# Low parts of split weights: an accumulating DMA in place of VectorE's subtraction, in a two-layer hybrid encoder

## The chip, the cores and the metric

The kernel runs on one core of one Trainium2 chip. The metric is the time of one execution on the device, in microseconds (us). Engines: TensorE (PE; its weight loads are PEld), VectorE (DVE), ScalarE (ACT), GpSimd (POOL) and SyncE (SP), which here only issues DMAs.

## The reference, cut to what matters

Two layers over 512 tokens of width 1024. Each layer is a half-step SwiGLU, a mixer of three parallel head groups, and a second half-step SwiGLU with a gated embedding, every one of them closed by a layer norm:

```
x = LN(a*x + 0.5 * (silu(x @ Wg) * (x @ Wu)) @ Wd)            # 1024 -> 2816 -> 1024
h = x @ W_in                                                  # retention | RG-LRU | gated delta rule
x = LN(a*x + concat(ret(h), lru(h), delta(h)) @ W_out)
x = LN(a*x + 0.5 * swiglu_2(x) + sigmoid(x @ W_g) * (p @ W_p))
```

Everything is float32, and all weights are inputs in HBM, each read once.

## The kernel before, in words

**Products.** TensorE multiplies in the rounded format F32R. To keep float32 precision each operand is split into a high part (the operand rounded to F32R) and a low part (the operand minus its high part), and a product is three matmuls: high by high, high by low, low by high. The kernel therefore needs both parts of every weight.

**Weights.** `jobs` lists 178 loads of up to 1 MB in the order of use. A load lands in a `raw` tile of [128, 2048] float32, of which there are two. It holds one or two units of up to 1024 columns, 354 units in all. `split_to` takes a unit from the raw tile to two slots of memory: `act` (line 215) writes the high part on ScalarE, `tt` (line 233) the low part by a subtraction on VectorE, or, inside the mixer, on GpSimd where the planner's clocks say that it ends sooner (`either`). When a load's last unit is split, the load after next is queued (`load_to(j + 2)`) and waits on SP's queue for its raw tile.

**Use.** `take` hands the next unit to a product and splits the one after it. In the gate and up products (`fm`, first half of `swiglu`) a unit is 24 matmuls of 512 columns. In the down product (`rows`, second half) a unit is 12 matmuls for tokens 0 to 255 and, `LAG` units later, 12 more for the others, so LAG + 1 units and their activations stay in memory. In the embedding (`embed`) ten units are taken in a row at 12 matmuls each, kept, and used a second time for the other tokens; the output projection of the mixer takes eight in the same way.

**Memory.** 40 slots of 4 KB per partition hold split weights (two slots a unit), activations and the mixer's tensors. A slot given back goes to the end of a queue. A write to it waits for its last reader.

**Order.** The mixer's scans and delta rules are threads (`spawn`) that are interleaved with the dense products by estimates of the engines' clocks (`clk`, `spend`). The tile framework then sets the order in each engine's queue; the queues are in order.

Of the kernel before, what the change touches and what calls it, by code (L numbers as in the profile page):

```python
# [20 lines left out]
LN_EPS = 1e-5  # L21
LAG = 7
NSPLIT = 2
# [10 lines left out]

# columns of the constant table
C_ID, C_U, C_V, C_STR, C_ONE, C_LV = 0, 128, 256, 384, 512, 640
# [4 lines left out]
NC_ = C_FR + 1  # L41
# columns of the vectors of one layer
V_GC, V_LC, V_LB, V_BA, V_BX, V_LAM, V_RN, V_GN, V_AL, V_DT, NV = 0, 36, 48, 51, 54, 57, 60, 62, 63, 69, 75


class Slots:
    """Equal pieces of memory, each given out and taken back by the kernel."""

# [19 lines left out]
class Halves:  # L68
    """Half slots: two tensors of 2 KB per partition in one slot."""

# [37 lines left out]
def tile_trunk(ctx: ExitStack, tc: tile.TileContext, a, out):  # L108
    nc = tc.nc
# [12 lines left out]

# [1 line left out]
    class Ctx:  # L124
# [28 lines left out]
    def place(e, t, ns):  # L153
        """The end of work of ns that can begin at t."""
        if e == "P" or INORDER:
            clk[e] = max(clk[e], t) + ns
            return clk[e]
        q = gaps[e]
        for i, (g0, g1) in enumerate(q):
            s = max(g0, t)  # L160
            if s + ns <= g1:
                del q[i]
                if g1 - s - ns > 50.0:
                    q.insert(i, (s + ns, g1))
                if s - g0 > 50.0:
                    if len(q) == q.maxlen:
                        q.popleft()
                        i -= 1
                    q.insert(max(i, 0), (g0, s))
                return s + ns  # L170
        s = max(ends[e], t)
        if s - ends[e] > 50.0:
            q.append((ends[e], s))
        ends[e] = s + ns
        return s + ns
# [3 lines left out]
    def later(f, *args):  # L179
        """Work that the next step of its thread does not wait for."""  # L180
        lazy[0] = True
        f(*args)
        lazy[0] = False

    def until(*aps):
        """The next step of the thread waits for these."""
        cur[0].t = max(cur[0].t, available("P", aps) - HOP)
# [13 lines left out]
    def begin(t=None):  # L201
        """What follows on the other engines waits for the tensor engine's work so far."""
        cur[0] = Ctx(clk["P"] if t is None else t, "P")
# [18 lines left out]
    def either(ns_v, ns_g):  # L222
        """The vector engine or GpSimd, whichever is done first."""
        return nc.gpsimd if max(clk["G"], cur[0].t) + ns_g < max(clk["D"], cur[0].t) + ns_v else None
# [30 lines left out]
    def pmm(out, lhsT, rhs, ns, start=True, stop=True):  # L255
        """A product of side work."""
        nc.tensor.matmul(out=out, lhsT=lhsT, rhs=rhs, start=start, stop=stop)  # L257
        spend("P", ns, [out], [lhsT, rhs])
# [55 lines left out]

# [1 line left out]
    cst = cpool.tile([128, C_LV], F32, name="cst")  # L316
# [20 lines left out]

# [1 line left out]
    jobs = []  # L339

    def job(src, parts):
        """src: a load of up to 8 KB per partition; parts: (first column, columns) of its units."""
        jobs.append((src, parts))
# [29 lines left out]
    def load_to(j):  # L373
        while st["loaded"] <= min(j, len(jobs) - 1):
# [15 lines left out]
            if st["loaded"] == 6:  # L390
                consts()
                spawn(rotary_tables())

    def split_to(i):
        while st["split"] <= min(i, len(order) - 1):
# [8 lines left out]
            for c0, c1 in [(0, n)] if st["split"] else [(0, 512), (512, n)]:  # L404
                act(hi[:, c0:c1], w[:, c0:c1])
                tt(lo[:, c0:c1], w[:, c0:c1], f32(hi[:, c0:c1]), SUB, either(70 + 1.04 * n, 90 + 2.0 * n) if in_mixer[0] else None)
            stock.append((hi, lo, cur[0].t))
# [8 lines left out]
    def take(ahead=1):  # L416
        i = st["taken"]
        if st["split"] <= i:
            wait_until(lambda: len(slots.free) >= 2 + spare[0] or not side)
        split_to(i)  # L420
        st["taken"] += 1
        hi, lo, t = stock.popleft()
        clk["P"] = max(clk["P"], t + HOP)
        if len(slots.free) >= 2 * ahead + spare[0]:
            split_to(i + ahead)
        return hi, lo

# [1 line left out]
    xh, xl = [None] * 4, [None] * 4  # L429

    def fm(dst, w, c0, c1):
        """128 features of x @ W, features on partitions, tokens c0..c1."""
        hi = w[0].rearrange("p (k c) -> p k c", k=8)
# [10 lines left out]
    def rows(acc, w, lh, ll, tiles, first, last, cs=(0, 1)):  # L444
        """One K tile of A @ W, tokens on partitions."""
        for t in tiles:
# [20 lines left out]
    def split_into(dst, col, src):  # L467
        """dst: [128, 2 (hi, lo), S]; src: [128, n] float32 in SBUF or PSUM"""
        act(dst[:, 0, col], src)
# [9 lines left out]

# [1 line left out]
    def load_gb(l, nm):  # L481
# [6 lines left out]
    def rsqrt(dst, src, add, mul=None):  # L488
        """dst = (src * mul + add) ** -0.5"""
        if mul is None:  # L490
# [19 lines left out]
    def norm(t, acc, c, gb, out=None, halves_done=None):  # L510
        """Layer norm of one tile of tokens, and its transpose, split."""
        x = xt[t]
# [56 lines left out]

# [1 line left out]
    def swiglu(l, nm, pend, out=None):  # L571
# [91 lines left out]

# [1 line left out]
    def conv(dst, p, taps, bias=None, before=None):  # L665
        """dst = causal convolution over tokens (free axis) of PSUM p; before: the 3 tokens ahead of it."""
        n = p.shape[1]
# [10 lines left out]
    def softplus(dst, src, n):  # L678
        """log(1 + exp(src)) of [128, n], by max(x, 0) + 2 atanh(e / (2 + e)), e = exp(-|x|)"""
        t = small.tile([128, 5, n], F32, tag=f"sp{n}", name="sp")  # L680
# [15 lines left out]
    def mixer(l, pend):  # L696
# [14 lines left out]

        # tokens on partitions: v_r, a, b
        wtm = [take() for _ in range(3)]
# [17 lines left out]
        def decays(half):  # L731
            """Decays of the delta rule, per token and head, of two tiles."""
            u = small.tile([128, 8, 12], F32, tag="sc", name="sc", bufs=4)
# [51 lines left out]
        def kv_part(i, w, half):  # L785
            """A half of the tokens of one tile of k (i < 3) or v of the delta rule."""
            wait_until(lambda: len(ps.free) >= 1)
# [20 lines left out]
        def delta(hp, half):  # L808
            """The gated delta rule of two heads over two tiles of 128 tokens."""
            while half and len(slots.free) < GUARD:  # L810
# [20 lines left out]

            # unit-norm keys
            until(kT[hp].ap[:, t0:t0 + 256])
# [43 lines left out]
            es.put()  # L877
            # approximate inverse by block doubling
            yield from room(ROOM_2)
# [17 lines left out]
            for i in range(n):  # L897
                yield
                # T (I - A_off T): the mask, with signs, picks I - A_off T out of (I + A) T
                p = yield from bk()  # L900
# [4 lines left out]
                yield  # L905
                # of T only the even blocks of columns change, of its transpose the odd ones
                w = LEVELS[i]
# [13 lines left out]
            for b in hb:  # L921
                b.put()
            # solve, and refine with the float32 matrix
            while (half, hp) not in there:
# [46 lines left out]
            yield  # L971
            # queries
            while qT[hp] is None:
# [24 lines left out]
            kk_.put()  # L998
            # state over the tiles
            p = yield from bk()  # L1000
# [49 lines left out]
            kt_.put()  # L1050
            # norm, gate
            sq = halves.get(F32)
# [28 lines left out]
        def lru():  # L1081
            """RG-LRU, channels on partitions."""
            yield from room(3)
# [53 lines left out]
        def retention():  # L1137
            """Retention, a state carried over the tiles of 128 tokens."""
            while not all(th.done for th in turns):
# [155 lines left out]

        # half of the tokens ahead of the other
        in_mixer[0] = True
# [90 lines left out]

        # output projection: the parts of the mixer as they are done
        acc = [None] * 4  # L1390
# [33 lines left out]

# [1 line left out]
    def embed(l, pend):  # L1426
# [43 lines left out]

# [1 line left out]
    def rotary_tables():  # L1472
# [40 lines left out]
        for c in (c1, c2, c3):  # L1513
            stt(ang, kh, -c, ang, MUL, ADD)
            stt(ang, kl, -c, ang, MUL, ADD)
            yield
        # the sine's argument lies within [-pi, pi]
        lim = 3.1415925
# [7 lines left out]

# [1 line left out]
    if True:  # L1528
# [136 lines left out]
```

## Time and profile before

| | us |
|---|---|
| timed runs, median of 2 | 2195.29 |
| timed runs, lowest and highest | 2194.08, 2196.50 |
| profiled execution, span from first to last instruction | 2196.0 |
| PE busy | 2170.8 |
| PEld busy | 1813.3 |
| DVE busy | 1081.6 |
| ACT busy | 741.1 |
| POOL busy | 221.1 |

The span of the profiled execution stands 0.7 us above the median, so sums are made against the span and then compared with the median. PE counts as busy from a matmul's start to its modelled end, so a busy PE is not one at its peak. The two mixers lie at about 350 to 690 us and 1440 to 1780 us; the stretches around them are the SwiGLUs and embeddings.

### The profile page before, as it was taken

How to read it: one execution, taken by the hardware profiler on the slowest of the kernel's cores; microseconds unless marked ns; L12 is line 12 of the kernel's file. 1: busy time of each engine (PE TensorE's matmuls, PEld its weight loads, DVE VectorE, ACT ScalarE, POOL GpSimd, SP SyncE). 2: the span in 40 equal slices, each digit the busy share in tenths (PEclk: the TensorE clock that was granted, in tenths of full speed). 3: DMA queues.
4: the chain of work that ended last, by engine and by line, in shares of the span. 5: the costliest groups of instructions: out<-in, count | busy, mean ns of one | idle time of the engine just before them, and what ended most of it. 6: DMA issues, size and time to landing. Idle time of an engine off the chain costs nothing.

```text
span 2196.0 us, 26879 instructions
## 1 busy us (share of the span) xinstructions
PE 2170.8 (99%) x11240; PEld 1813.3 (83%) x11240; DVE 1081.6 (49%) x1769; ACT 741.1 (34%) x1152; POOL 221.1 (10%) x170
## 2 busy tenths in 40 slices
PE   8999999999999999999999999999999999999998
PEld 7888888977888888888898888888778888888887
DVE  7323336887857432332453333278878574232324
ACT  5322223555523322232232222235565143222320
POOL 1000001233311100000000000012433110000000
PEclk9999999999979999999999999999999899999999
DMA  7222342210223322233232222421102233222330
GB/s 271 96 77 77 115 135 79 76 47 20 85 87 115 115 77 77 77 114 132 80 115 81 91 79 99 142 87 58 46 21 104 68 124 107 88 85 77 115 115 39
DMA packets 40889, 202.77 MB, mean 92 GB/s; under 512 B 3904, under 2 KB 5952, under 8 KB 26560
## 3 DMA queue, kind: packets, MB, share of 16 engines
q1 hardware_dynamic: 40768, 201.06, 26.5%
q8 instruction: 88, 1.44, 0.3%
q14 instruction: 33, 0.27, 0.0%
HBM read 198.95 MB, written 2.10 MB: 92 GB/s over the span
## 4 chain that ended last, share of the span: by engine, by line
PE 89%; DVE 6%; ACT 2%; POOL 1%; issue 1%; DMA 0%; SPq 0%; DVEq 0%; POOLq 0%; ACTq 0%
PE p L303 82%; PE p L257 6%; DVE s L233 3%; DVE s L237 2%; PE p L261 1%; ACT s L215 1%; ACT L215 0%; POOL s L233 0%; POOL fs L497 0%; POOL rk L497 0%; DMA raw<-in_wgu_dram 0%; POOL rq L497 0%; DVE s L1125 0%; DVE x L237 0%; DVE sp L237 0%
## 5 line engine op out<-in xcount | busy, mean ns | idle before, releaser
L303 PE MATMUL p<-s,s 128*128 128x512 f32 (+2 forms) x9024 | 2006.9, 380 | 7.5 <-ACT s L215 7.2
L303 PEld LDWEIGHTS p<-s,s 128*128 128x128 f32 x9024 | 1619.3, 189 | 309.2 <-ACT s L215 7.8
L233 DVE TENSOR_TENSOR s<-raw,s 128x1024 fp32r<-128x1024 f32 (+2 forms) x345 | 426.3, 1243 | 640.0 <-PE p L303 297.3
L215 ACT ACTIVATE s<-raw 128x1024 fp32r<-128x1024 f32 (+2 forms) x355 | 369.3, 1051 | 786.9 <-PE p L303 654.3
L215 ACT ACTIVATE s<-p 128x256 fp32r<-128x256 f32 (+6 forms) x464 | 190.3, 454 | 337.0 <-PE p L303 166.6
L233 DVE TENSOR_TENSOR s<-s,p 128x512 f32<-128x512 f32 (+3 forms) x176 | 102.9, 589 | 270.2 <-PE p L303 246.2
L215 ACT ACTIVATE s<-s 128x512 fp32r<-128x512 f32 (+5 forms) x205 | 112.6, 555 | 254.1 <-DVE s L233 155.3
L497 POOL TENSOR_TENSOR rs<-rs,half_neg 128x1 f32<-128x1 f32 x24 | 33.9, 1412 | 1487.1 <-DVE rs L242 1487.1
L257 PE MATMUL p<-s,s 128*128 128x64 f16 (+5 forms) x1504 | 158.6, 253 | 5.1 <-DVE s L233 3.4
L233 DVE TENSOR_TENSOR s<-s,s 128x512 fp32r<-128x512 f32 (+2 forms) x141 | 92.2, 660 | 50.0 <-ACT s L215 49.5
L257 PEld LDWEIGHTS p<-s,s 128*128 128x128 f32 (+1 forms) x688 | 95.8, 206 | 20.9 <-issue 5.5
L237 DVE SCALAR_TENSOR_TENSOR s<-p,vecs,s 128x255 f32<-128x255 f32 (+4 forms) x128 | 70.2, 551 | 15.7 <-PE p L261 7.7
L233 DVE TENSOR_TENSOR s<-p,s 128x256 fp32r<-128x256 f32 (+4 forms) x124 | 53.5, 453 | 20.2 <-ACT s L215 10.3
L215 ACT ACT_TABLE_LOAD x42 | 53.9, 1283 | 5.0 <-DVE tails L248 3.6
L257 PEld LDWEIGHTS <-s 128*128 128x128 f16 x816 | 35.2, 98 | 20.0 <-issue 10.4
L233 DVE TENSOR_TENSOR s<-p,lvm 128x512 f16<-128x512 f32 x72 | 47.0, 680 | 4.1 <-PE p L257 4.1
L233 POOL TENSOR_TENSOR s<-s,cst 128x512 f32<-128x512 f32 x26 | 37.8, 1455 | 93.8 <-DVE s L233 74.2
L237 DVE SCALAR_TENSOR_TENSOR x<-p,x 128x512 f32<-128x512 f32 x48 | 31.1, 681 | 27.4 <-PE p L303 27.3
L237 DVE SCALAR_TENSOR_TENSOR x<-x,rs,s 128x1024 f32<-128x1024 f32 (+1 forms) x25 | 30.6, 1237 | 2.8 <-POOL rs L497 2.7
L261 PE MATMUL p<-cst,s 128*128 128x128 f32 x172 | 30.9, 281 | 0.8 <-DVE s L233 0.8
L215 ACT ACTIVATE s<-p,vecs 128x256 f32<-128x256 f32 (+1 forms) x48 | 27.5, 587 | 9.8 <-PE p L303 9.8
L237 DVE SCALAR_TENSOR_TENSOR x<-x,mv,s 128x1024 f32<-128x1024 f32 (+1 forms) x25 | 30.7, 1231 | 0.0
(100 smaller groups left out, 593.5 us busy)
## 6 DMA issues: line engine op xcount, KB each, us to landing
raw<-in_wgu_dram SPq DMA_DIRECT2D x87, 1024.0 KB, 4.8
raw<-in_ffn_w_down_dram SPq DMA_DIRECT2D x44, 1024.0 KB, 4.9
raw<-in_win_fm_dram SPq DMA_DIRECT2D x24, 1024.0 KB, 4.8
raw<-in_w_out_dram SPq DMA_DIRECT2D x8, 1024.0 KB, 4.9
raw<-in_ple_w_gate_dram SPq DMA_DIRECT2D x8, 1024.0 KB, 4.9
s<-in_xT_dram SPq DMA_DIRECT2D x8, 256.0 KB, 6.6
x<-in_x_dram SPq DMA_DIRECT2D x4, 512.0 KB, 6.0
s<-in_ln_ffn_g_dram SPq DMA_DIRECT2D x4, 512.0 KB, 4.2
```

Of the source, the lines that this page charges most:

```text
L215: nc.scalar.activation(out=out, in_=in_, func=func, **kw)
L233: (eng or nc.vector).tensor_tensor(out=out, in0=in0, in1=in1, op=op)
L237: nc.vector.scalar_tensor_tensor(out=out, in0=in0, scalar=scalar, in1=in1, op0=op0, op1=op1)
L257: nc.tensor.matmul(out=out, lhsT=lhsT, rhs=rhs, start=start, stop=stop)
L261: nc.tensor.transpose(out, in_, idn)
L303: nc.tensor.matmul(out=out, lhsT=lhsT, rhs=rhs, start=start, stop=stop)
L497: nc.gpsimd.tensor_tensor(out=dst, in0=dst, in1=e, op=POW)
```

## The change

Three edits. First, from the third unit on, ScalarE writes the negated high part into the low slot (`scale=-1.0`), and a DMA issued by GpSimd adds the raw weight to it in place (`accum_op=ADD`); the planner books 1.0 us of GpSimd and 3.0 us more until the result is there. Only the first two units keep VectorE's subtraction. Second, `LAG` is 5 in place of 7. Third, `take` splits one unit further ahead when no side thread runs and at least six slots are free. Comments and docstrings are left out too, which shifts line numbers.

```diff
-LAG = 7
+LAG = 5
...
+    def add_by_dma(out, in_):
+
+        nc.gpsimd.dma_start(out=out, in_=in_, accum_op=ADD)
+        spend("G", 1000.0, [], [out])
+        t = clk["G"] + 3000.0
+        for b in blocks(out):
+            ready[b] = (t, "Q")
+        if not lazy[0]:
+            cur[0].t = max(cur[0].t, t)
+
     def split_to(i):
...
                 act(hi[:, c0:c1], w[:, c0:c1])
-                tt(lo[:, c0:c1], w[:, c0:c1], f32(hi[:, c0:c1]), SUB, either(70 + 1.04 * n, 90 + 2.0 * n) if in_mixer[0] else None)
+                if st["split"] < 2:
+                    tt(lo[:, c0:c1], w[:, c0:c1], f32(hi[:, c0:c1]), SUB)
+                else:
+                    act(lo[:, c0:c1], w[:, c0:c1], scale=-1.0)
+                    add_by_dma(lo[:, c0:c1], w[:, c0:c1])
...
         if len(slots.free) >= 2 * ahead + spare[0]:
             split_to(i + ahead)
+            if not side and len(slots.free) >= 6:
+                split_to(i + ahead + 1)
```

Counted over the program: splits on ScalarE go from 355 to 707 instructions, those on VectorE from 345 to 3, those on GpSimd from 10 to none, and GpSimd issues 352 DMAs where it issued none.

In an instruction's name s_120_1391 the first number counts slots handed out (high and low part of a unit follow each other), p_ is a PSUM bank, raw a raw weight tile. ScalarE's queue in the middle of the first gate and up products, before:

```order
L215 ACTIVATE s_104_1222<-p_27_1168 128x512
L215 ACTIVATE s_118_1360<-raw 128x1024
L215 ACTIVATE s_99_1161<-s_104_1222 128x512
L215 ACTIVATE s_120_1391<-raw 128x1024
L215 ACTIVATE s_110_1288<-p_29_1234 128x512
L215 ACTIVATE s_124_1426<-raw 128x1024
```

The same place after:

```order
L215 ACTIVATE s_106_1256<-p_27_1199 128x512
L215 ACTIVATE s_117_1361<-raw 128x1024
L215 ACTIVATE s_101_1193<-s_106_1256 128x512
L215 ACTIVATE s_120_1398<-raw 128x1024
L215 ACTIVATE s_121_1399<-raw 128x1024
L215 ACTIVATE s_112_1324<-p_29_1267 128x512
L215 ACTIVATE s_122_1428<-raw 128x1024
```

Each high part is now followed by the write of its negated copy into the low slot. In both, the unit whose high part is s_120 is split ahead of the silu of bank p_29 and first used for bank p_35, 120 matmuls after the one for which that silu waits.

GpSimd's queue in the first mixer, where the delta rule's keys are normalized (rk), before (sc and cst are small constants and decays):

```order
L497 TENSOR_TENSOR rk<-rk,half_neg 128x4
L242 TENSOR_SCALAR sc<-sc 128x12
L497 TENSOR_TENSOR rk<-rk,half_neg 128x4 x2
L233 TENSOR_TENSOR s_253_3413<-raw,s_252_3412 128x1024
L233 TENSOR_TENSOR s_238_2991<-s_238_2991,cst 128x512
L233 TENSOR_TENSOR s_260_3602<-raw,s_259_3601 128x1024
```

The same place after:

```order
L513 TENSOR_TENSOR rk<-rk,half_neg 128x4
L396 DMA s_243_3401<-raw 128x1024
L396 DMA s_245_3462<-raw 128x1024
L513 TENSOR_TENSOR rk<-rk,half_neg 128x4
L242 TENSOR_SCALAR sc<-sc 128x12
L233 TENSOR_TENSOR s_239_3107<-s_239_3107,cst 128x512
L396 DMA s_248_3547<-raw 128x1024
L396 DMA s_250_3584<-raw 128x1024
```

Issues of accumulating DMAs, each of which waits for ScalarE's second split, now stand between the powers that the delta rule waits for; the subtractions of raw tiles are gone from this queue.

## Rows read from the trace of the kernel before

**Rows 1.** The page's busy times: us (share of the span) and instructions of each engine.

```profile
PE 2170.8 (99%) x11240; PEld 1813.3 (83%) x11240; DVE 1081.6 (49%) x1769; ACT 741.1 (34%) x1152; POOL 221.1 (10%) x170
```

**Rows 2.** The chain that ended last: shares by line; start us, us, what.

```profile
by line: PE p L303 82.4%; PE p L257 5.5%; DVE s L233 3.3%; DVE s L237 2.3%; PE p L261 1.5%; ACT s L215 1.3%; issue 0.8%; ACT L215 0.4%; POOL s L233 0.3%; POOL fs L497 0.3%; POOL rk L497 0.3%; DMA raw<-in_wgu_dram 0.3%; POOL rq L497 0.2%; DV
...
9.99 350.53 PE p L303 x1624
...
406.26 1.05 POOL rk L497
...
1785.70 402.60 PE p L303 x1776
```

**Rows 3.** Timeline of a dense stretch: start us, us, engine, line, operands, count.

```profile
99.69 30.54 PE L303 MATMUL p<-s,s 128*128 128x512 f32 x134
```

**Rows 4.** Groups by line and shape: count | busy us, mean ns | idle before.

```profile
L233 DVE TENSOR_TENSOR s<-raw,s 128x1024 fp32r<-128x1024 f32 x337 | 419.7, 1252 | 599.0 <-PE p L303 297.3 <-ACT s L215 237.9 <-issue 52.9
L215 ACT ACTIVATE s<-raw 128x1024 fp32r<-128x1024 f32 x347 | 363.2, 1058 | 737.5 <-PE p L303 608.3 <-DVE s L233 34.8 <-DMA raw<-in_wgu_dram 20.6
```

**Rows 5.** Windows: length, busy PE, PEld, DVE, ACT, POOL; granted clock, DMA share, GB/s.

```profile
100.00:150.00 50.00, 50.00 (x222) 41.40 (x221) 16.16 (x18) 14.32 (x19) 0.00 (x0) 1.00 0.24 84
350.00:425.00 75.00, 75.00 (x539) 70.53 (x538) 65.23 (x156) 41.15 (x75) 16.68 (x13) 1.00 0.25 88
425.00:600.00 175.00, 170.33 (x1266) 137.67 (x1265) 143.15 (x293) 94.57 (x194) 61.17 (x49) 1.00 0.13 45
600.00:650.00 50.00, 49.65 (x218) 39.77 (x217) 27.67 (x70) 11.56 (x23) 8.61 (x7) 0.73 0.32 106
1515.00:1690.00 175.00, 170.31 (x1269) 137.84 (x1269) 143.25 (x297) 95.04 (x195) 61.16 (x49) 1.00 0.14 48
1690.00:1750.00 60.00, 59.66 (x284) 48.34 (x283) 35.50 (x86) 15.44 (x29) 9.13 (x6) 0.83 0.28 97
```

**Rows 6.** Windows, raw-tile instructions: length, busy DVE, ACT, POOL; clock, DMA share, GB/s.

```profile
350.00:425.00 75.00, 13.28 (x11) 12.34 (x12) 2.44 (x1) 1.00 0.25 88
425.00:600.00 175.00, 12.66 (x10) 16.15 (x16) 10.18 (x4) 1.00 0.13 45
600.00:650.00 50.00, 8.59 (x7) 5.94 (x6) 0.00 (x0) 0.73 0.32 106
```

**Rows 7.** Waits of SP's queue: us in total, times, longest.

```profile
SPq L387 <- DVE s L233: 1641.3, 164, 23.6
```

**Rows 8.** The page's DMA queue and issues: KB each, us to landing.

```profile
q1 hardware_dynamic: 40768, 201.06, 26.5%
...
raw<-in_wgu_dram SPq DMA_DIRECT2D x87, 1024.0 KB, 4.8
...
out_dram<-x SPq DMA_DIRECT2D x3, 512.0 KB, 2.6
```

**Rows 9.** Timeline of the first 25 us.

```profile
18.33 3.89 ACT L215 ACTIVATE s<-raw 128x1024 fp32r<-128x1024 f32 x4
...
19.40 2.45 DVE L233 TENSOR_TENSOR s<-raw,s 128x1024 fp32r<-128x1024 f32 x2 [0.52 <-ACT s L215]
```

**Rows 10.** Timeline of the start of the first layer's embedding.

```profile
678.25 3.94 SPq L387 DMA_DIRECT2D raw<-in_ple_w_gate_dram  x2
...
684.18 11.84 PE L303 MATMUL p<-s,s 128*128 128x512 f32 x51
...
695.04 1.06 ACT L215 ACTIVATE s<-raw 128x1024 fp32r<-128x1024 f32 x1 [6.33 <-DMA raw<-in_ple_w_proj_dram]
...
698.29 1.23 DVE L233 TENSOR_TENSOR s<-raw,s 128x1024 fp32r<-128x1024 f32 x1 [0.27 <-ACT s L215]
```

**Rows 11.** Timeline in the first mixer, VectorE and GpSimd.

```profile
414.02 0.21 DVE L237 SCALAR_TENSOR_TENSOR s<-tails,vecs,s 128x1 f32<-128x1 f32 x1
...
420.04 2.44 POOL L233 TENSOR_TENSOR s<-raw,s 128x1024 fp32r<-128x1024 f32 x1 [4.84 <-ACT s L215]
...
420.52 1.98 DVE L237 SCALAR_TENSOR_TENSOR s<-tails,vecs,s 128x1 f32<-128x1 f32 x1
```

## The prediction

> **What bounds the kernel now.** I began with the busy times: TensorE 99% of the span, VectorE 49%, ScalarE 34%, GpSimd 10% [rows 1]. VectorE, the engine that the change relieves, is half idle, so its total says little; where it is waited for matters. The chain that ended last shows that. Matmuls take 82.4, 5.5 and 1.5% of it, and four pieces are matmuls without a break for 340 to 400 us (from 10, 697, 1111 and 1786 us; the first and last stand in [rows 2]), 1486 us of 2196 together. There a piece of 134 matmuls takes 30.54 us, 228 ns each [rows 3]; a unit of 24 matmuls therefore takes 5.47 us, and VectorE is busy 16 of 50 us [rows 5]. Relief for VectorE is worth nothing in these four stretches, and a change can only lose there.
>
> What is left to win lies in the mixers. The windows show TensorE busy 170.33 of 175 us in the middle of the first and 170.31 of 175 in the second, and 49.65 of 50 and 59.66 of 60 in the stretches behind them: 10 us idle in all [rows 5]. In the two later stretches the granted clock is 0.73 and 0.83, a mixture of the 1.2 and 2.4 GHz levels. TensorE loses there (1 - 0.73) x 50 = 13.5 and (1 - 0.83) x 60 = 10.2 us, 24 together, by its slower pace. Before the clock fell TensorE had gone through the mixer's short, waiting products. So some 34 us, 1.5% of the span, are within reach, even if all mixer waits went.
>
> **What the change takes off VectorE.** 342 subtractions at 1.25 us [rows 4] are 428 us, two fifths of VectorE's time. By place: 13.28 of its 65.23 us in 350 to 425, 12.66 of 143.15 in 425 to 600, 8.59 of 27.67 in 600 to 650; and from GpSimd 10.18 of 61.17 us in the middle window [rows 5, 6]. In the middle of the mixer VectorE is 82% busy and sheds a tenth; in the stretch behind it, where the clock is low, it sheds a third. Of the 34 us I take half, -17: the scans that fill VectorE's remaining 130 us wait for one another as before, but the splits that stand between two of their steps are gone. The ends are 0 (those steps wait for other things) and -34.
>
> **What it adds to ScalarE.** 352 more splits at 1.06 us [rows 4] are 373 us; ScalarE goes from 741 to some 1114 us, half the span. In 425 to 600 it has 94.57 us and gets 16 more, in 600 to 650 11.56 and 6 more [rows 5, 6]. It stays below two thirds busy everywhere, and in gate and up products below 25 of 50 us (14.32 before, and nine splits more). I cost it at nothing there; the cover is that a split stands 120 matmuls, 27 us, ahead of its first use.
>
> **What it adds to the DMA engines.** The trace of before has no accumulating DMA, so I bound the engines' time A for one of 512 KB. The weights' queue spends 26.5% of the span on 201.06 MB [rows 8]: 0.265 x 2196 / 201.06 = 2.89 us per MB, 1.5 us per 512 KB moved once. That is the lower end. An addition reads two operands, 3.0 us, and that is the value I take; if two reads and a write were each a stream of their own it would be 4.6 us, the upper end. A unit also needs its half of a 1 MB load, 1.5 us. Together a unit asks for 3.0, 4.5 or 6.1 us of the DMA engines while TensorE works 5.47 us on it. At 3.0 the engines go from a quarter busy [rows 5] to some 80%, and TensorE still hides them. The tipping point is A = 3.95.
>
> **How late a low part is.** The time L from issue to landing is at least 2.6 us, what a plain 512 KB transfer to HBM takes [rows 8]. At most I put 2.44 us for the issue, GpSimd's time for touching such a tile itself [rows 11], and two full 1 MB transfers of 4.8 us [rows 8]: 12 us. I take 6: one 4.8 us transfer, since two operands of 512 KB are read, and 1.2 us of issue. In a gate or up product a raw tile goes round in 4.8 (load) + 4 x 1.06 (four ScalarE instructions for two units) + 6.0 = 15 us, and with two tiles TensorE allows the four units' 21.9 us. So the load waits longer for its tile, for a DMA instead of VectorE as in [rows 7], and nobody waits for the load until L passes about 12. Cost: nothing, at either end almost.
>
> **Where the cover is thin.** First, the start. Unit 2's low part was ready at 20.6 us, after the first of VectorE's two subtractions from 19.40 [rows 9]. Afterwards ScalarE ends both its parts at about 20.4, and the addition lands 6 us later, 26.4. In the changed order TensorE first uses this part about 100 matmuls after the start at 10, some 22.8 us at the full pace. That is +4 us; the ends are 0 (L = 2.6) and +10. Second, the embeddings, which take ten units in a row at 12 matmuls, 2.73 us. The last unit of the first embedding was split by 698.29 + 1.23 = 699.5 [rows 10] and is wanted nine units after the start at about 685: 709.6. Its margin is 10 us. Each time round of a raw tile gets later by L + 1.06 - 1.25 = 5.8 us, and two or three of them lie in this run: 11.6 to 17.4, so a stall of 1.5 to 7. Against that stand the freer slots, from which splits start earlier. I take +2 for each of two embeddings, +4; the ends are 0 and +14. The output projections take eight units the same way, but the mixer's end gives them time.
>
> **The smaller edits.** `LAG` 5 takes 2 x 2.73 = 5.5 us of matmuls away from behind the layer norm of the first tokens, once in each down product, three times with work behind it. VectorE sheds 13 us in the stretch behind the product [rows 6], which hides it; without that cover it is at most +16. The same edit frees six slots, two units and their activations; the deeper prefetch can use them.
>
> **GpSimd's queue.** It now issues 352 DMAs, each waiting for ScalarE. What is queued behind them in the mixer are the powers that normalize keys, queries and decays. They are on the chain: 17 steps of rk, rq and fs from 406 to 1701 us, each about 1.05 us [rows 2]. My sum takes no delay for these, because the change also takes the 2.44 us subtractions out of the same queue; the price otherwise is the second rival's.
>
> Two engines also meet at the SBUF port. VectorE's smallest operation of one form took 0.21 us alone and 1.98 us when it stood beside a 2.44 us subtraction on GpSimd [rows 11]. The Trainium skill, page "SBUF — State Buffer", section "SBUF: two separate sides", says that a DMA issued from GpSimd has its descriptors written by GpSimd itself, which is shut out of a port pair while VectorE holds it; by this rule the additions in the mixer, where VectorE is 82% busy, would be late by the VectorE instruction that stands there; at the 1.98 us of that row for each of the chain's 17 steps of GpSimd named below it would add 34 us to the second rival. The row shows the pair blocking VectorE; no run of before shows it blocking a DMA.
>
> **Sum.** 2196 - 17 + 4 + 4 = 2187 us, 9 us under the span and 8 under the median. Its own range, from the bounds of the terms (-34 to 0, and 0 to +20 without the unlikeliest combination), is 2165 to 2215. About 2% of the time, 44 us, is what a measurement of this kernel can tell from no change, so this counts as none.
>
> **Rivals.** *The DMA engines become the bound.* If an addition costs 4.6 us, each of the 264 units of the SwiGLUs takes 6.1 us in place of 5.47: +0.61 x 264 = +161, 2357 us. It decides from A = 3.95. For it: no row prices an addition. Against it: it needs a separate time for the write, which the queue's row for plain copies already includes. Chance 0.09.
>
> *GpSimd's queue becomes the delta rule's clock* (the slower side). A power that arrives behind an issue waits for ScalarE's 1.06 us and an issue of 1.2 us, 2.3 in all; 17 such steps give +39, and the mixers then win nothing: 2196 + 8 + 39 = 2243. Behind two issues, 2 x 1.06 + 2.44 = 4.6 us each, it is +78, 2282. Within 2% it stays below (44 - 8) / 17 = 2.1 us per step. For it: the changed order has pairs of issues between two powers, and these steps are on the chain. Against it: a step is late only if it comes due while an issue stands ahead of it, and in the middle of a mixer there are only some 16 splits in 175 us [rows 6]. Chance 0.16.
>
> *The mixers give everything back*: -34 and no new wait, 2162, or down to 2147 if faster scans also let the products around them run at the full clock. For it: VectorE and GpSimd together shed 23 us in the middle window. Against it: ScalarE is in the same steps and gets more. Chance 0.10.
>
> That the change does nothing at all I leave out: in its order all but three low parts come from GpSimd's DMAs.
>
> **How the numbers follow.** Forecast 0.65, rivals 0.09, 0.16 and 0.10. Faster by over 2% is below 2151, the lower half of the last rival: 0.05. Slower by over 2% is the first rival and five eighths of the second: 0.19. The rest, 0.76, is within 2%. The range goes from 2150 to 2245: it leaves out the first rival, the dearer half of the second and a little of the third, just under 0.2.
>
> **What would show it.** VectorE near 650 us, ScalarE near 1110, and a second DMA queue of the software kind whose share of the span gives A directly (352 x 3.0 / 2196 = 48%); the landing time of the additions gives L. In the dense windows TensorE should keep about 222 matmuls in 50 us; if it falls behind there and waits for DMAs, the first rival holds. The mixers are right if they end earlier with a higher granted clock, and wrong if the chain shows issues or longer waits ahead of rk, rq and fs. What would make the forecast wrong most cheaply is an L above 12 us, with which the raw tiles run late in every product.

## The result: 5% slower, and the profile after

The changed kernel takes 2309.92 us (2306.32 to 2313.52) against 2195.29: +115 us, ratio 1.052, interval 1.048 to 1.056. Its profiled execution has a span of 2304.5 us.

The page's busy times and DMA queues of the changed kernel, in the form of [rows 1] and [rows 8]:

```profile
PE 2198.5 (95%) x11240; PEld 1831.0 (79%) x11240; DVE 674.9 (29%) x1429; ACT 1071.1 (46%) x1510; POOL 483.0 (21%) x510
...
q0 software_dynamic: 50688, 183.62, 42.8%
q1 hardware_dynamic: 40768, 201.06, 25.7%
```

VectorE lost 407 us and ScalarE gained 330. TensorE's busy time rose by 28 us, its idle time by 81. It ran the same 11240 matmuls, at a granted clock of 0.978 where the kernel before had 0.988. The second queue is the additions': 42.8% of 2304.5 us over 352 is 2.80 us of the DMA engines each.

Issues and what landed from them, KB each and median us:

```profile
s<-raw POOLq DMA_DIRECT2D x346, 512.0 KB, 5.5
raw<-in_wgu_dram SPq DMA_DIRECT2D x87, 1024.0 KB, 5.7
```

An addition lands 5.5 us after its issue in the median, near the 6 of the prediction, and the loads' 4.8 us have become 5.7. The same by place, from the view of the line that issues them; first 100 to 250 us (gate and up products), then 425 to 600 (the mixer's middle):

```profile
L396 POOL DMA_DIRECT2D s<-raw x26: 859/859/862, 106.1 to 247.1; - x26
...
DMA to landing us min/median/max: 4.5/7.7/12.4
...
L396 POOL DMA_DIRECT2D s<-raw x12: 866/914/1176, 436.9 to 596.1; - x12
...
DMA to landing us min/median/max: 4.5/4.6/6.9
```

Windows (length; busy PE, PEld, DVE, ACT, POOL; granted clock, DMA share, GB/s), those of [rows 5] and one more, in the down product:

```profile
100.00:150.00 50.00, 50.00 (x222) 41.39 (x222) 6.82 (x10) 22.34 (x28) 6.88 (x8) 1.00 0.83 195
266.00:300.00 34.00, 31.48 (x137) 25.49 (x138) 0.00 (x0) 15.39 (x16) 6.54 (x8) 1.00 0.98 254
350.00:425.00 75.00, 63.93 (x370) 56.73 (x369) 41.18 (x98) 33.69 (x58) 16.51 (x17) 0.91 0.61 143
425.00:600.00 175.00, 162.87 (x1251) 135.96 (x1251) 124.81 (x287) 111.82 (x214) 55.96 (x55) 0.94 0.31 75
600.00:650.00 50.00, 49.90 (x266) 40.90 (x265) 25.33 (x60) 19.94 (x31) 12.80 (x13) 0.93 0.55 135
```

In the gate and up products TensorE still runs 222 matmuls in 50 us, with the DMA engines 83% busy. In the down product's first stretch they are 98% busy and TensorE waits. In the mixer it is busy 162.87 of 175 us, where it was 170.33. The time is lost everywhere but in the stretches that hold most of the additions.

SP's queue and then ScalarE, what they waited for, us in total, times, longest:

```profile
SPq L387 <- DMA s<-raw: 2010.7, 195, 43.7
...
ACT s L215 <- DMA raw<-in_wgu_dram: 227.1, 41, 11.8
ACT s L215 <- DMA raw<-in_ffn_w_down_dram: 188.6, 21, 12.2
...
ACT s L215 <- DMA raw<-in_win_tm_dram: 37.0, 4, 9.9
ACT s L215 <- DMA raw<-in_ple_w_gate_dram: 36.4, 4, 10.0
...
ACT s L215 <- DMA raw<-in_win_fm_dram: 30.0, 7, 7.2
```

Loads wait for the additions that still read the raw tile, where they waited for VectorE [rows 7], and ScalarE now waits for loads: 37 + 227 + 189 + 36 + 30 us in the five lines of weights. Those waits become TensorE's where it takes units fast. Here is the start of the first down product, in the timeline (start us, us, engine, line, operands, count, and the idle time before with what ended it):

```profile
266.84 11.37 PE L303 MATMUL p<-s,s 128*128 128x512 f32 x48 [1.38 <-DMA s<-raw]
...
272.83 7.69 ACT L215 ACTIVATE s<-raw 128x1024 fp32r<-128x1024 f32 x8 [10.18 <-DMA raw<-in_ffn_w_down_dram]
...
279.89 20.49 PE L303 MATMUL p<-s,s 128*128 128x512 f32 x89 [1.68 <-DMA s<-raw]
```

Five to six units are taken in a row at 2.73 us. ScalarE waits 10 us for a load, TensorE for two additions. Before, it ran through this stretch without a pause [rows 2].

### The profile page after: what moved, and what is told of

Same layout as the page of the kernel before. It is cut to its first block, busy times and chain, and to the rows that moved or that the text cites. A ratio compares the mean times of both kernels' runs of the same rounds, so it can differ in the third digit from the quotient of the medians.

```text
span 2304.5 us, 27876 instructions
## 1 busy us (share of the span) xinstructions
PE 2198.5 (95%) x11240; PEld 1831.0 (79%) x11240; DVE 674.9 (29%) x1429; ACT 1071.1 (46%) x1510; POOL 483.0 (21%) x510
## 3 DMA queue, kind: packets, MB, share of 16 engines
q0 software_dynamic: 50688, 183.62, 42.8%
## 5 line engine op out<-in xcount | busy, mean ns | idle before, releaser
L303 PE MATMUL p<-s,s 128*128 128x512 f32 (+2 forms) x9024 | 2019.3, 381 | 40.9 <-ACT s L215 23.8
L215 ACT ACTIVATE s<-raw 128x1024 fp32r<-128x1024 f32 (+2 forms) x707 | 709.5, 1047 | 867.0 <-PE p L303 263.6
L396 POOL DMA_DIRECT2D s<-raw x352 | 306.8, 881 | 1466.1 <-ACT s L215 1368.9
L215 ACT ACTIVATE s<-p 128x256 fp32r<-128x256 f32 (+4 forms) x464 | 191.8, 450 | 201.8 <-PE p L257 66.9
L257 PE MATMUL p<-s,s 128*128 128x128 f16 (+5 forms) x1484 | 160.9, 254 | 8.1 <-ACT s L215 4.5
L233 DVE TENSOR_TENSOR s<-s,s 128x512 fp32r<-128x512 f32 (+3 forms) x139 | 89.2, 647 | 198.0 <-ACT s L215 196.2
L237 DVE SCALAR_TENSOR_TENSOR s<-p,vecs,s 128x255 f32<-128x255 f32 (+5 forms) x128 | 69.6, 551 | 20.0 <-ACT s L215 11.4
L237 DVE SCALAR_TENSOR_TENSOR s<-s,p 64x64 f32<-64x64 f32 (+1 forms) x32 | 13.6, 450 | 98.6 <-PE p L303 51.0
L257 PE MATMUL p<-s 128*128 128x128 f32 (+1 forms) x216 | 29.4, 301 | 9.3 <-DVE s L233 7.8
```

The lines of the kernel that those rows point to most:

```text
L215: nc.scalar.activation(out=out, in_=in_, func=func, **kw)
L233: (eng or nc.vector).tensor_tensor(out=out, in0=in0, in1=in1, op=op)
L237: nc.vector.scalar_tensor_tensor(out=out, in0=in0, scalar=scalar, in1=in1, op0=op0, op1=op1)
L396: nc.gpsimd.dma_start(out=out, in_=in_, accum_op=ADD)
```

## The experiments

Each is timed against the kernel before on the same chip; differences are to that kernel's median in the same comparison (2193 to 2197 us).

**The smaller edits.** First the kernel before with the second and third edit, and no addition by DMA:

```diff
-LAG = 7
+LAG = 5
...
             split_to(i + ahead)
+            if not side and len(slots.free) >= 6:
+                split_to(i + ahead + 1)
```

> The kernel before with LAG 5 and the deeper prefetch, but with VectorE's subtractions. If the loss of 114 us comes from the additions (theories of GpSimd's queue, of the raw tiles and of the DMA engines alike): 2185 to 2205 us, no change. If the smaller edits carry it, because the shorter LAG uncovers the layer norms or the slots go to the wrong units: 2280 or more.

2235.17 us, +42, ratio 1.019 (1.016 to 1.021), between the two brackets. More than a third of the loss has nothing to do with the additions. The two edits apart:

> The kernel before with LAG 5 alone. LAG 5 and the deeper prefetch together cost 41 us, nearly all in the two mixers. If the shorter LAG carries that, because the layer norms ahead of the mixers stand uncovered: 2225 to 2240 us. If the prefetch carries it: 2188 to 2200.

> The kernel before with the deeper prefetch alone. If the shorter LAG carries the 41 us: 2188 to 2200 us. If the prefetch carries it, because units split early hold slots that the mixer's threads want: 2220 to 2240.

`LAG` 5 alone gives 2260.05 us, +65 (ratio 1.029, 1.028 to 1.031); the prefetch alone 2198.55, +4 (1.002, 1.001 to 1.003). So the prefetch costs next to nothing and wins back some 25 us of what the shorter `LAG` loses. The windows with `LAG` 5 alone show where that is:

```profile
350.00:425.00 75.00, 75.00 (x533) 70.61 (x532) 66.22 (x152) 39.10 (x73) 16.62 (x12) 1.00 0.25 85
425.00:600.00 175.00, 152.07 (x1107) 122.75 (x1105) 129.26 (x258) 88.81 (x181) 56.42 (x49) 0.94 0.10 32
600.00:650.00 50.00, 50.00 (x233) 41.74 (x233) 25.92 (x62) 11.86 (x24) 5.30 (x4) 0.71 0.14 48
```

In 350 to 425 us, the layer norm's stretch, TensorE is busy 75.00 of 75 us as before. The expectation's reason, uncovered layer norms, is wrong. The loss stands in the middle of the mixer, 152.07 us busy where it was 170.33, and at a granted clock of 0.94 where it was 1.00. The page of this run has both halves of it:

```profile
PE 2202.4 (97%) x11240; PEld 1844.0 (82%) x11240; DVE 1088.6 (48%) x1769; ACT 752.7 (33%) x1158; POOL 210.7 (9%) x170
```

For the same matmuls TensorE is busy 32 us longer than before, at a granted clock of 0.973 in place of 0.988, and idle 33 us longer (span 2260.2 us). Half of the loss is waiting, the other half a slower pace.

**ScalarE's splits against VectorE's relief.** The changed kernel with the DMA left out and all else kept, and the same with `LAG` 7 and the old prefetch:

```diff
-        nc.gpsimd.dma_start(out=out, in_=in_, accum_op=ADD)
         spend("G", 1000.0, [], [out])
```

> The changed kernel with both ScalarE splits, but no addition is issued; the low parts stay the negated high parts. If the additions cost the time, by GpSimd's queue, by the raw tiles that they hold or by the DMA engines' time: 2170 to 2205 us. If ScalarE's 352 extra splits cost it (other ScalarE work queued behind them): 2270 to 2310.

> The same without any addition issued: low parts stay the negated high parts; LAG 7, no deeper prefetch. It shows what the relief of VectorE is worth with nothing against it but ScalarE's extra splits. The prediction's term was -17 us, thus 2176; if relief is worth nothing: 2188 to 2200; if ScalarE's splits cost something in the mixers: 2205 or more.

2234.91 us, between its brackets and the same as the 2235.17 with VectorE's subtractions; and 2219.47, +24, with `LAG` 7 (1.011, 1.009 to 1.014). The exchange of VectorE's 407 us for ScalarE's second splits is worth nothing with the new settings, and with the old ones it costs 24 us. The relief was predicted at -17 and the splits at nothing; no run has the one without the other.

**The additions alone**, the changed kernel with `LAG` 7 and without the deeper prefetch:

> The changed kernel with LAG 7 and without the deeper prefetch: the additions alone. If their cost adds to that of the smaller edits: 2193 + 75 = 2268 us (2255 to 2280). If the prefetch and the freed slots hide part of the additions' latency, as the prediction assumed: 2285 or more. If the two are the same loss in the mixers twice counted: 2290 to 2310.

2347.00 us, +152 (1.069, 1.065 to 1.072). The smaller edits, a loss by themselves, save 37 us here. With `LAG` 7 the additions cost 2347 - 2219 = 128 us, with the edits 2310 - 2235 = 75.

**Powers behind issues.** A power on GpSimd is replaced by a constant from a short VectorE instruction; in the first pair the planner is told, in the other three runs it is not, so that the order stays:

```diff
-        nc.gpsimd.tensor_tensor(out=dst, in0=dst, in1=e, op=POW)
+        nc.vector.tensor_scalar(out=dst, in0=dst, scalar1=0.0, scalar2=0.05, op0=MUL, op1=ADD)
```

> The changed kernel without the powers on GpSimd: the reciprocal roots are replaced by a constant that one short VectorE instruction writes. GpSimd's additions stand ahead of none of them then. Read against the same edit on the kernel before. Theory of GpSimd's queue (powers stand behind issues that wait for ScalarE and for a load): most of the 114 us goes, the difference to its partner falls below 50 us. Theory of the raw tiles (the loads come late whatever GpSimd does): the difference stays at 85 to 115 us.

> The kernel before with the same constants in place of the powers, the partner of the run above. Both theories: the powers themselves are on the chain of before with 17 steps of about 1.05 us and a few layer norms, so 2160 to 2190 us.

The changed kernel takes 2254.57 us without powers, its partner 2206.44: a difference of 48, which looked like the queue theory. But the partner is slower than before by 13 with less work, so the order had moved, and the pair does not tell.

> The changed kernel with each power replaced by a constant written by VectorE, this time with the planner still booking it on GpSimd, so that the order stays that of the changed kernel almost row for row. Theory that powers queued behind issues cost time: 2255 to 2275 us, some 40 us less than 2310 and clearly more than its partner without additions gains. Theory that the powers only cost what they cost anywhere, and the earlier pair differed by its order: 2290 to 2305.

> The kernel before with the same edit, order kept. Both theories: the powers' own microsecond off the chain in the mixers, 2175 to 2195 us.

> The changed kernel without additions issued (low parts stay negated high parts) and with the powers' place taken by the constant. The gain against the 2235 us of the run without additions is what the powers cost with nothing ahead of them. Theory of powers behind issues: a gain of 0 to 15 us, 2220 to 2235. Theory that powers cost the same with and without additions: a gain as large as in the changed kernel.

With the order kept the powers are worth 29 us in the changed kernel (2280.86, between the brackets of both theories), 24 without additions (2211.41 against 2234.91) and 12 in the kernel before (2181.65). With the settings of the change, additions ahead of the powers cost some 5 us, about what the comparison can tell. As the explanation of the loss the theory of GpSimd's queue fell here.

**The raw tile.** The addition's source is the high part, in a slot of its own, so that the raw tile is free once ScalarE has read it:

```diff
-                    add_by_dma(lo[:, c0:c1], w[:, c0:c1])
+                    add_by_dma(lo[:, c0:c1], f32(hi[:, c0:c1]))
```

> The changed kernel with the addition's source changed: it adds the high part, which has a slot of its own, in place of the raw weight (the low parts become zero, so low parts of weights are left out of the result). Issues, landings, bytes and TensorE's waits for landings stay; only the raw tile comes free as soon as ScalarE has read it, not at the landing. Theory of the raw tiles (two tiles held through the landing make loads late, and with them ScalarE, GpSimd's issues and what stands behind them): 2235 to 2265 us, near the 2235 of the run without additions. Theory of GpSimd's queue by itself (a power waits for ScalarE's 1 us and an issue of 0.9 us): 2285 to 2310. Theory of the DMA engines' time: 2300 to 2320.

> The run above with the powers replaced by a constant as well. If raw tiles and GpSimd's queue are all that the additions cost: 2200 to 2225 us. If the landing itself or the DMA engines' time costs TensorE something in the bursts: 2235 to 2255, like the 2254.6 us without the powers alone.

2280.59 us, 29 less than the changed kernel, outside both brackets. ScalarE's waits for loads in the SwiGLUs fall to a third:

```profile
ACT s L215 <- DMA raw<-in_ffn_w_down_dram: 92.7, 20, 6.6
...
ACT s L215 <- DMA raw<-in_wgu_dram: 54.6, 22, 5.5
```

What TensorE waited for in the dense products, in the changed kernel (the first two lines) and with the tile free:

```profile
PE p L303 <- ACT s L215: 23.8, 5, 6.3
PE p L303 <- DMA s<-raw: 16.9, 10, 3.3
...
PE p L303 <- DMA s<-s: 19.3, 8, 3.0
...
PE p L303 <- ACT s L215: 6.7, 2, 5.6
```

The waits for landings stay, 17 and 19 us. Those for ScalarE fall from 23.8 to 6.7, about what the start of each run has: three waits of 4.6 to 6.3 us are gone.

Without powers 2240.92, inside its second bracket; but that run belongs to the pair whose order had moved and says no more than it. Three raw tiles, with 38 slots to make room:

```diff
-NSLOT = 40
+NSLOT = 38
...
-    rpool = ctx.enter_context(tc.tile_pool(name="raw", bufs=2))
+    rpool = ctx.enter_context(tc.tile_pool(name="raw", bufs=3))
...
-                load_to(j + 2)
+                load_to(j + 3)
```

> The changed kernel with three raw tiles in place of two and, to make room, 38 slots in place of 40. Against the run with 38 slots and two tiles. Theory of the raw tiles: 35 to 60 us faster than that. Theory of GpSimd's queue by itself or of the DMA engines' time: within 15 us of it.

> The changed kernel with 38 slots, the partner of the run with three raw tiles. All theories: a little slower than with 40, since fewer units are split ahead: 2310 to 2340 us.

2261.33 us with three tiles, 2298.53 with two: 37 us, as the theory of the raw tiles has it. Two slots fewer cost nothing, the run is 11 us faster than with 40; that expectation missed.

**The landing.** TensorE reads the high part in the low part's place, so no matmul waits for an addition:

```diff
-        lo = w[1].rearrange("p (k c) -> p k c", k=8)
+        lo = w[0].rearrange("p (k c) -> p k c", k=8)
```

(and likewise in `rows` and `tm_part`).

> The changed kernel with TensorE reading the high part of each weight in the low part's place (low parts of weights left out of the result). The additions are issued and land as before and the raw tiles are held for them, but no matmul waits for a landing. Theory of the landing wait (TensorE waits for DMAs in the bursts): 25 to 45 us less than 2310. Theory that loads and GpSimd's queue carry it all: 2295 to 2312.

2450.26 us, 140 slower than the changed kernel, which no theory had. With no reader of the sum the framework is free to order ScalarE's second splits and the additions otherwise. That it put them later, so that the raw tiles came free later, is inferred from the waits, not read from the queues. ScalarE, what it waited for:

```profile
ACT s L215 <- DMA raw<-in_wgu_dram: 588.6, 85, 13.3
ACT s L215 <- DMA raw<-in_ffn_w_down_dram: 277.8, 30, 12.3
```

589 and 278 us, where the changed kernel has 227 and 189. It doesn't price the landing.

**Bytes or issues.** Each addition cut to 64 of 1024 columns:

```diff
-                    add_by_dma(lo[:, c0:c1], w[:, c0:c1])
+                    add_by_dma(lo[:, c0:c0 + 64], w[:, c0:c0 + 64])
```

> The changed kernel with each addition cut to the first 64 of its 1024 columns (the other columns of the low part stay negated high parts). As many issues, each still waiting for ScalarE's second split, and the same queue; the bytes fall to a sixteenth, and with them the landing and the time that a raw tile is held for it. Theory that the size of the addition costs the time (landing, tile and DMA engines): 2230 to 2250 us, near the 2235 without additions. Theory that issuing them costs it (the issue's place in GpSimd's queue, waits for a semaphore): 2280 to 2310.

2240.95 us, +45. Its issues, its queue, and its windows at the first down product and embedding:

```profile
q0 software_dynamic: 50688, 11.56, 6.2%
...
s<-raw POOLq DMA_DIRECT2D x352, 32.0 KB, 2.2
...
L396 POOL DMA_DIRECT2D s<-raw x352: 837/859/1434, 21.3 to 2178.2; - x176
...
258.00:292.00 34.00, 34.00 (x152) 28.16 (x151) 0.00 (x0) 15.85 (x16) 6.99 (x9) 1.00 0.61 191
695.00:755.00 60.00, 59.45 (x270) 48.81 (x269) 15.28 (x26) 37.54 (x47) 20.61 (x20) 1.00 0.48 132
```

As many issues, of the same 0.86 us and in the same queue, cost 6 us more than none (2240.95 against 2234.91, and 4 when each is set against its own reference). The bytes cost the other 69. In the down product, where the changed kernel's DMA engines stood at 98%, they are 61% busy and TensorE 34.00 of 34.

**Additions for the gate and up weights alone**, with `LAG` 7, the old prefetch, and VectorE's subtraction for all other weights:

```diff
-                if st["split"] < 2:
+                if st["split"] < 2 or j not in gu:
```

(`gu` holds the numbers of the gate and up loads.)

> Additions by DMA for the gate and up weights alone, where TensorE takes a unit every 5.47 us; VectorE's subtraction, LAG 7 and the old prefetch everywhere else. Theory that the additions are hidden in the dense products and cost time only where units are taken twice as fast and in the mixers: 2192 to 2210 us. Theory that they also cost time in the gate and up products: 2230 or more. In no theory does it gain, since VectorE is not waited for there.

2197.95 us, +2, ratio 1.001 (1.000 to 1.003). Half of the additions, at the same price for the DMA engines (22.3% of 2197.2 us over 174 is 2.82), cost next to nothing in sum:

```profile
100.00:150.00 50.00, 50.00 (x222) 41.42 (x221) 8.13 (x12) 26.82 (x34) 9.46 (x11) 1.00 0.86 206
600.00:650.00 50.00, 49.65 (x273) 40.65 (x272) 34.55 (x85) 15.02 (x30) 9.55 (x7) 0.97 0.35 116
...
26.42 23.80 PE L303 MATMUL p<-s,s 128*128 128x256 f32 x147 [1.95 <-DMA s<-raw]
...
1110.84 19.41 PE L303 MATMUL p<-s,s 128*128 128x256 f32 x122 [3.42 <-ACT s L215]
```

In the middle of the gate and up products the DMA engines are 86% busy and VectorE 8 of 50 us, and TensorE's 222 matmuls are unmoved. At the edges the additions do cost something: TensorE waits at the start and, in layer 2, at the first units of gate and up, which are taken for half of the tokens at a time. The stages of the table below take 379.0, 304.1, 415.1, 367.8, 314.3 and 410.6 us in this run: the SwiGLUs are 8 us slower than before, and the mixers together 7 us faster, with the same work in them. Behind the first mixer, in 600 to 650 us, the granted clock is 0.97 where it was 0.73 [rows 5]. So the tie owes something to luck of order. No run that does all of the work beats the kernel before, and with the exchange worth nothing the runs point to none that would.

## Why the prediction was wrong

The sum of the steps, in medians: 2193 before, 2235 with the smaller edits, 2235 with ScalarE's splits in the place of VectorE's subtractions, 2241 with small additions issued, 2281 with whole additions that leave the raw tile free, 2310 with the tile held. By stage, from the last aggregate of one layer norm in the timeline to the last of the next, us:

| stage | before | smaller edits | no additions | 64 columns | tile free | after |
|---|---|---|---|---|---|---|
| SwiGLU 1, layer 1 | 376.3 | 377.3 | 375.7 | 376.8 | 388.0 | 390.4 |
| mixer, layer 1 | 313.9 | 330.5 | 325.6 | 329.6 | 338.8 | 334.3 |
| embedding, SwiGLU 2 | 414.5 | 415.5 | 416.3 | 416.5 | 422.8 | 431.4 |
| SwiGLU 1, layer 2 | 363.2 | 363.5 | 364.1 | 364.1 | 368.9 | 384.3 |
| mixer, layer 2 | 311.3 | 330.3 | 328.9 | 329.0 | 336.6 | 329.8 |
| embedding, SwiGLU 2 | 410.6 | 410.9 | 413.6 | 413.8 | 420.4 | 427.7 |

**What held.** That TensorE bounds the dense stretches and VectorE's time is worth nothing there; that the gate and up products hide the additions (the last experiment); A, predicted 3.0 and measured 2.80 us; L, predicted 6 and measured 5.5 in the median, though 7.7 in the gate and up products; the start, predicted +4: in the changed kernel TensorE waits 3.25 us for the first additions, where its matmuls ran on without a break from 9.99 us [rows 2]; this is the row of it in the timeline:

```profile
26.90 23.46 PE L303 MATMUL p<-s,s 128*128 128x256 f32 x139 [3.25 <-DMA s<-raw]
```

**The step that failed: "where the cover is thin".** The additions were put at +8 us, the start and two embeddings, and measured 75 (2310 against 2235). The step compared the DMA engines' 4.5 us for a unit with TensorE's 5.47 and found 80% busy. But where a unit is taken in 12 matmuls, 2.73 us, it asks more of the DMA engines than that: 1.5 + 2.8 = 4.3 us. There they are asked for more than TensorE's time without A having to pass 3.95, and the window of the down product shows them 98% busy. The prediction priced such places by L alone, and named the embeddings alone. It left out the first units of each down product, which are taken at the same 2.73 us until `LAG` is reached, and the first units of gate and up in layer 2. (The output projections, which it passed over, did no harm: the bytes cost 4.7 and 0.8 us in the mixers.) The table has the price: 13.6, 14.9, 20.2 and 13.9 us (after less 64 columns) in the four stages with a down product, 63 of the 69 us of the bytes. This is the first rival's mechanism at another place; its price of 161 us and its condition were for gate and up, where it doesn't hold.

Of the 16.9 us for which TensorE waits for landings (the lines at the raw tile), 3 lie at the start and 13 in the four down products. In the embeddings it waits by another path than the one that was priced. Here are the first embedding and the start of layer 2 in the changed kernel's timeline, with a window over the former:

```profile
748.96 2.56 PE L303 MATMUL p<-s,s 128*128 128x512 f32 x10 [0.46 <-DMA s<-raw]
749.20 3.90 ACT L215 ACTIVATE s<-raw 128x1024 fp32r<-128x1024 f32 x4 [9.81 <-DMA raw<-in_wgu_dram]
...
757.17 2.06 ACT L215 ACTIVATE s<-p 128x512 f32<-128x512 f32 x4
...
757.82 17.56 PE L303 MATMUL p<-s,s 128*128 128x512 f32 x70 [6.29 <-ACT s L215]
...
1171.30 13.87 PE L303 MATMUL p<-s,s 128*128 128x256 f32 x91 [4.58 <-ACT s L215]
...
745.00:770.00 25.00, 18.24 (x73) 14.25 (x72) 2.48 (x4) 14.32 (x16) 8.12 (x6) 0.86 0.77 202
```

The low part, priced at 2 us, is late by 0.46 us. The other 6.29 us are a wait for the gate's sigmoids, which read the finished banks and stand in ScalarE's queue behind splits; those wait 9.81 us for a load, and the load for its raw tile. The second embedding repeats it with 5.51 us. So a late load stops TensorE without a late low part, when other work stands behind the split in ScalarE's queue.

Waiting is not all. The page of the run with 64 columns:

```profile
PE 2182.2 (98%) x11240; PEld 1822.9 (81%) x11240; DVE 678.7 (30%) x1429; ACT 1084.2 (48%) x1512; POOL 486.7 (22%) x510
```

With the whole additions TensorE is idle 51 us longer than here and, for the same matmuls, busy 16 us longer: its granted clock is 0.978 against 0.986, and it fell in the stretches around such waits, as to 0.86 in the window above, a mixture of the 1.2 and 2.4 GHz levels. The waits beyond the two paths lie at the layer norms, of which one stands below, and in the mixers. The prediction had the clock only as something to win.

The raw tile is some 29 to 37 of those 69 us, the term taken as "nothing, at either end almost". Its reckoning of 15 us for a round against 21.9 was for four units at 5.47 us; in a burst four units last 10.9. The prediction had named late raw tiles as the cheapest way to be wrong, but only from L = 12; they came late with a median of 5.5. The rest, about 40, comes with the bytes even when the tile is free: TensorE waits 19 us for landings, and the mixers are 17 us slower than with 64 columns. How much of that is slower clock, loads that share the engines, or order alone was not told apart.

**"The smaller edits", priced at zero to +16:** measured +42, a `LAG` of 65 less 25 from the prefetch. The cover named was the right question at the wrong place: the layer norms stayed covered, and the mixers' middle lost. Why a shorter `LAG` slows a mixer is open. What the runs show is that the same mixer takes from 304 to 343 us when nothing of its work differs, only its order and with it the granted clock: 304.1 us in layer 1 with additions for gate and up alone, 313.9 before, 342.8 with `LAG` 5 alone.

**"Of the 34 us I take half":** measured 0 with the settings of the change and a loss of 24 with the old ones. Either the work that VectorE shed in the mixer was not what TensorE waited for, or ScalarE's second splits, priced at nothing, took it back; no run tells which.

**The second rival**, powers of rk, rq and fs behind issues, had the right sign by a wrong mechanism: 2243 to 2282 for 17 delayed steps. Layer norms' powers (rs) do stand behind issues at a few places, as the timeline behind the first down product shows:

```profile
367.38 0.14 DVE L242 TENSOR_SCALAR rs<-mv 128x1 f32<-128x1 f32 x1
...
370.00 2.96 ACT L215 ACTIVATE s<-raw 128x1024 fp32r<-128x1024 f32 x3 [4.75 <-DMA raw<-in_win_fm_dram]
372.31 1.81 POOL L396 DMA_DIRECT2D s<-raw  x2 [7.79 <-ACT s L215]
373.82 0.90 POOL L513 TENSOR_TENSOR rs<-rs,half_neg 128x1 f32<-128x1 f32 x1
...
376.10 0.66 PE L261 MATMUL p<-cst,x 128*128 128x128 f32 x4 [2.27 <-DVE rs L242]
```

The input is ready at 367.5 us; an issue that waits for ScalarE and a load stands ahead, and the power starts at 373.8, where TensorE then waits for it. But with the order kept, such delays are worth some 5 us in all. As to the page "SBUF — State Buffer" of the Trainium skill (section "SBUF: two separate sides"), which the prediction cites, the trace does not show its rule delaying the additions: in the mixer, with VectorE 71% busy, an issue took 914 ns against 859 in the dense stretch, and its addition landed sooner, 4.6 against 7.7 us.

## What to carry to other kernels

Set what a change asks of a shared resource against the fastest rate at which any stretch consumes, not against the longest stretch's rate: the additions fit a unit of 5.47 us and not one of 2.73. A low mean (DMA engines a quarter busy) says nothing of these bursts, and a buffer held 5 us longer must be reckoned there as well. Look also at what stands behind a late step in the same queue: the sigmoids waited for a load that they don't use. And test bundled edits singly: a constant that looked free cost 65 us, and its companion repaid 25.

## What the runs showed of the hardware

An addition from SBUF to SBUF of 512 KB costs the 16 DMA engines 2.80 us, nearly twice the 1.5 us of a plain load of as many bytes, and one of 32 KB 6.2% x 2236.9 / 352 = 0.39 us, more than twice a sixteenth of it; both take as many packets (50688). Issuing either takes GpSimd 0.86 us. The landing differs by stretch: 4.6 us in the mixer at a DMA share of 0.31, 7.7 with up to 12.4 in the gate and up products at 0.83.
